# A two-layer diffusion trunk on one core: last squares summed by TensorE, two items tile by tile, low parts in halves, and a new order of the second attention

## The chip, the core and the metric

The kernel runs on one core of a Trainium2 chip. Its engines work side by side and wait for each other through semaphores: TensorE (PE in the profile: matrix products into eight PSUM banks), VectorE (DVE) and ScalarE (ACT) for elementwise work, GpSimd (POOL) likewise, and SyncE (SP), which issues most DMAs. Each engine takes its instructions strictly in the order in which they were written. The metric is the device time of one execution in microseconds, 2162.36 us (median of three runs, 2161.0 to 2166.12).

## The reference

256 latent tokens and 256 context tokens of width 1024 pass two layers in fp32. A layer is a half-step SwiGLU feed-forward (width 2816), then three mixers side by side (latent attention "MLA" with 8 heads, differential attention with 8 heads, pooling over windows 2 to 16) whose outputs are gated, summed and projected, then a second half-step feed-forward. Cut to what matters here:

```
def rmsnorm(x, g):
    y = x32 * rsqrt(mean(x32 * x32, axis=-1) + EPS);  return y * g
for l in range(2):
    x = x + 0.5*m[2] * swiglu(rmsnorm(x, g0)*(1+m[1]) + m[0], *ffa)      # h (context) alike
    sx = mixer_streams(rmsnorm(x, g1)*(1+m[4]) + m[3], ...)              # keys of h and x together
    x = x + m[5] * mixer_output(sx, keys_x, ...)                         # h only in layer 0
    x = x + 0.5*m[8] * swiglu(rmsnorm(x, g2)*(1+m[7]) + m[6], *ffb)      # h only in layer 0
return rmsnorm(x, final_g)
```

What follows turns on the line between two parts: every norm needs the sum of squares of all 1024 channels of a token, and the next products can start only when the normed values are there.

## The kernel before

Activations lie transposed: eight tiles `X[k]` of 128 channels x 512 tokens, columns 0 to 255 the latent stream (X), 256 to 511 the context stream (H). Every product is made of three passes in a reduced fp32 format (`mm3`, line 301): an operand is split into a high part and a low part (`hi`, `lo`; `uh`, `ul`), and high x high, high x low and low x high are summed in PSUM. One weight block of 128x128 with one stream of 256 columns is thus three matmuls.

Weights come as 406 chunks of 128x1024 (eight blocks each) in the order of use. For each chunk (`Weights.split`, from line 140) SP loads `w`, ACT writes `hi` (line 152), and GpSimd or VectorE (by the flag `on_pool`) subtracts to get `lo` (line 156). A ring of four chunks limits how far this runs ahead.

The parts of a layer meet in `boundary` (from line 466). Half of the last product is made for both streams; the last four output tiles are made first for H, then for X, from the same held weights. Every finished tile is added to `X[k]` on VectorE (line 619 or 1404), squared on ACT and accumulated into `acc` on GpSimd (`sqacc`, from line 357); only the last tile's square is added by VectorE. `stat` (line 381) sums `acc` over the partitions on TensorE into `pst`; a square root and a reciprocal follow, `bcast` (line 396) spreads the result by two transposes into the PSUM tile `rB`, and `modulate` (lines 409 to 419) makes `uh` and `ul` for each of the eight tiles (a DVE, an ACT and a DVE instruction). The statistics of H come early, while X is still being made. After the last X tile, the next part's first items (`head()`) run for H: `fg` and `fu` of two feed-forward slices, or `dk0`, `dq0` and the values `dv0` of the attention (tiles `it`, `it`, `vi`). Item 0 runs alone over its eight blocks, then comes the statistic of X, then item 1, with `bcast` of X in its middle; then the other H items, and at last all items for X.

There are four such boundaries: into the attention of layer 0, into its second feed-forward, into layer 1's first feed-forward, into the attention of layer 1. The next ones, into layer 1's last feed-forward and to the end, use other code.

The mixing part walks over twelve attention units in layer 1: eight differential ones (head pair j, query tile qt), then four of MLA. A unit's scores (`a1`, four PSUM banks `sc`) and softmax (`soft`: four maxima on DVE, four exponentials `pe` on ACT) are written at once; the rest of the queue of each engine is set by hand in `SCHEDULE` (from line 44), one string per layer, one field between bars behind each unit. In it `N` is a step of normalising, `T` the transposes of the oldest pending unit, `V` its product with the values, `P` and `D` send low parts to GpSimd or VectorE, and names are fillers: projections (`dk2`, `cq1`, `q5`, `kr`), gate products (`g41`: output tile 4, branch 1), statistics (`ls`, `sq`, `st`), norms (`nk0`, `dn3`), pooling (`p1`, `pp1`, `pj1`). The four score banks, `tr`, `po`, `it` and `gt` tiles all come from the same ring of eight banks.

Of the kernel before, what the change touches and what calls it, by code (L numbers as in the profile page):

```python
# [17 lines left out]
D = 1024  # L18
KD = 8
T = 512  # L20
# [5 lines left out]
X_, H_ = 0, 1  # L26
XC, HC = slice(0, 256), slice(256, 512)
# [28 lines left out]
)  # L56


# [26 lines left out]
class Weights:  # L85
# [54 lines left out]
    def split(self, n, parts, copy):  # L140
        k, nc = self.k, self.k.nc
        hi = k.wpool.tile([128, CW], F32R, tag="hi", name=f"hi{n}", bufs=RING)
        lo = k.wpool.tile([128, CW], F32R, tag="lo", name=f"lo{n}", bufs=RING)
        if n in self.early:
            d = self.early.pop(n)
            nc.sync.dma_start(hi.bitcast(F32), d[:, 0, :])
            nc.sync.dma_start(lo.bitcast(F32), d[:, 1, :])
            self.hi[n], self.lo[n] = hi, lo
            return
        raw = k.raw_tile(f"w{n}")  # L150
        nc.sync.dma_start(raw, self.stream[n])
        copy(hi, raw)  # L152
        eng = nc.gpsimd if k.pool_split(n) else nc.vector
        for p in range(parts):
            c = slice(p * CW // parts, (p + 1) * CW // parts)
            eng.tensor_tensor(out=lo[:, c], in0=raw[:, c], in1=hi[:, c].bitcast(F32), op=ALU.subtract)  # L156
        self.hi[n], self.lo[n] = hi, lo
# [2 lines left out]
        floor = self.c if self.floor is None else min(self.floor, self.c)  # L160
        self.prefetch(floor + self.look)

    def prefetch(self, n, parts=1, copy=None):
        while self.done < NSPLIT and self.done <= n:
            self.split(self.done, parts, copy or self.k.nc.scalar.copy)
            self.done += 1
# [24 lines left out]
class Kernel:  # L191
# [274 lines left out]
    def boundary(self, l, i, specs, xs, update, head, func):  # L466


        nc = self.nc
        self.norm_begin(l, i)  # L470
        ng = 4
        cols = ALLC
        for dm, p in self.gemms(specs, xs, cols, range(KD - ng)):
            update(dm, p, cols)
            self.sqacc(dm, cols)
        self.preload(AF.Sqrt)
        W = self.W
        was, self.on_pool = self.on_pool, True
        W.hold()
        g = range(KD - ng, KD)  # L480
        blks, banks = {}, {}
        for dm in g:
            banks[dm] = self.ps("dn")
            blks[dm] = self.gemm(banks[dm][:, HC], specs(dm), xs, HC)
            update(dm, banks[dm], HC)
            self.sqacc(dm, HC, nc.vector if dm == KD - 1 else None)
        mids = (None, lambda: (self.bcast(H_), self.mod_list(H_, (0, 1))),
                lambda: self.mod_list(H_, (4, 5)), lambda: self.mod_end())
        ends = ((), (2, 3), (6, 7), ())
        for n, dm in enumerate(g):  # L490
            self.gemm(banks[dm][:, XC], blks[dm], xs, XC, mids[n])
            update(dm, banks[dm], XC)
            self.sqacc(dm, XC, nc.vector if dm == KD - 1 else None)
            if n == 0:
                self.stat(H_)
            self.mod_list(H_, ends[n])
            W.release(blks[dm + 1][0] if dm + 1 < KD else None)
        W.hold()
        items = head()

        def xstat():
            self.stat(X_)
            self.preload(func)
        for n, it in enumerate(items):
            it.mm(H_, lambda: (self.bcast(X_), self.mod_list(X_, range(KD)), self.mod_end()) if n == 1 else None)
            if n == 0:
                xstat()
        two = [it for it in items if not isinstance(it, Kernel.VItem)][:2]
        rest = [it for it in items if it not in two]
        preps = [it.prep(X_) for it in two]  # L510
        blks = [[] for _ in two]
        for k in range(KD):
            for (out, specs, xs, cols), bs in zip(preps, blks):
                b = specs[k] if not isinstance(specs[k][0], str) else W.take(specs[k])
                bs.append(b)
                self.mm3(out, b[:2], tuple(x[:, cols] for x in xs[k]), k == 0, k == KD - 1)
        for n, it in enumerate([None] + rest):
            if it:
                it.mm(X_)
            W.release(rest[n].blks[0] if n < len(rest) else None)  # L520
            self.run_later()
            for x in (it,) if it else two:
                x.finish()
        self.on_pool = was
# [39 lines left out]
    class FFN:  # L564
# [7 lines left out]
        def head(self):  # L572
            return [Kernel.FItem(self, f, up) for f in range(2) for up in (False, True)]
# [36 lines left out]
        def specs(self, fs):  # L610
            return lambda dm: [(self.down, self.l, f * 128, ((dm * 128, 128),)) for f in fs]

        def update(self, dm, p, cols):
            K, nc = self.K, self.K.nc
            m = 3 * self.i + 2
            for s in (X_, H_):
                if SC[s].start >= cols.start and SC[s].stop <= cols.stop:
                    x = K.X[dm][:, SC[s]]
                    nc.vector.scalar_tensor_tensor(out=x, in0=p[:, SC[s]], scalar=K.mod(self.l, m, s, dm), in1=x,  # L619
                                                   op0=ALU.mult, op1=ALU.add)  # L620
# [1149 lines left out]
```

## Time and profile before

| | us |
|---|---|
| median of three runs | 2162.36 |
| the profiled execution | 2161.61 |
| its span in the trace | 2159.8 |
| busy in the span: PE, DVE, ACT, POOL | 2120.6, 1370.3, 899.7, 772.2 |

TensorE is busy for 98% of the span. What any change of order can give back is the rest, and the stretches in which its granted clock is at the lower of its two levels (the mean over the execution is 0.991 of full speed). The profile's table by stretches shows where both lie; the list of waits says what PE waited for; the chain of waits and the engines' timelines say why that came late.

### The profile page before, as it was taken

How to read it: one execution, taken by the hardware profiler on the slowest of the kernel's cores; microseconds unless marked ns; L12 is line 12 of the kernel's file. 1: busy time of each engine (PE TensorE's matmuls, PEld its weight loads, DVE VectorE, ACT ScalarE, POOL GpSimd, SP SyncE). 2: the span in 40 equal slices, each digit the busy share in tenths (PEclk: the TensorE clock that was granted, in tenths of full speed). 3: DMA queues.
4: the chain of work that ended last, by engine and by line, in shares of the span. 5: the costliest groups of instructions: out<-in, count | busy, mean ns of one | idle time of the engine just before them, and what ended most of it. 6: DMA issues, size and time to landing. Idle time of an engine off the chain costs nothing.

```text
span 2159.8 us, 31295 instructions
## 1 busy us (share of the span) xinstructions
PE 2120.6 (98%) x12032; PEld 1824.9 (84%) x12032; DVE 1370.3 (63%) x2016; ACT 899.7 (42%) x1529; POOL 772.2 (36%) x561
## 2 busy tenths in 40 slices
PE   9999999999999999999999999999999999999998
PEld 5888888977887788888888898888889888999998
DVE  6665655456656799468758745544534776667755
ACT  4433233345565533432212243332333557555544
POOL 0333324322475411555545544333343347301000
PEclk9999999999999999999999999999999999999999
DMA  7577767264322466245444515786664552455653
GB/s 265 184 292 278 256 265 273 86 217 142 113 93 80 150 234 234 88 145 181 172 166 166 175 69 209 294 299 237 264 246 147 205 185 79 166 200 191 229 183 115
DMA packets 119241, 408.91 MB, mean 189 GB/s; under 512 B 13234, under 2 KB 16946, under 8 KB 119092
## 3 DMA queue, kind: packets, MB, share of 16 engines
q1 hardware_dynamic: 103252, 354.48, 46.7%
q10 hardware_dynamic: 15840, 52.44, 6.2%
q8 instruction: 94, 1.54, 0.3%
q14 instruction: 55, 0.45, 0.1%
HBM read 348.67 MB, written 58.20 MB: 188 GB/s over the span
## 4 chain that ended last, share of the span: by engine, by line
PE 86%; DVE 6%; ACT 4%; issue 1%; DMA 1%; POOL 1%; ACTq 0%; DVEq 0%; SPq 0%; POOLq 0%
PE dn L301 22%; PE fu L301 19%; PE fg L301 19%; PE gt L301 8%; PE it L301 5%; PE br L301 5%; PE vi L301 2%; ACT pe L806 1%; DVE ul L419 1%; PE fg L1578 1%; PE fu L1578 1%; PE pa L1508 1%; PE tr L853 1%; PE sc L1118 1%; DMA X<-X 1%
## 5 line engine op out<-in xcount | busy, mean ns | idle before, releaser
L156 POOL TENSOR_TENSOR lo<-w,hi 128x1024 fp32r<-128x1024 f32 x204 | 530.4, 2603 | 701.3 <-ACT hi L152 652.9
L152 ACT CAST hi<-w 128x1024 fp32r<-128x1024 f32 x359 | 374.8, 1049 | 579.2 <-DMA w<-in_stream 237.6
L271 DVE CUSTOM_DVE_ANT_0 junk<-a,cvec 128x1024 bf16<-128x1024 f32 x224 | 400.5, 1788 | 3.7
L301 PE MATMUL dn<-hh,hi 128*128 128x512 f32 (+1 forms) x800 | 272.7, 341 | 0.0
L301 PE MATMUL dn<-hl,hi 128*128 128x512 f32 (+1 forms) x800 | 272.2, 340 | 0.0
L301 PE MATMUL dn<-hh,lo 128*128 128x512 f32 (+1 forms) x800 | 272.2, 340 | 0.0
L156 DVE TENSOR_TENSOR lo<-w,hi 128x1024 fp32r<-128x1024 f32 x155 | 190.5, 1235 | 127.9 <-ACT hi L152 125.5
L301 PE MATMUL fg<-ul,hi 128*128 128x512 f32 (+2 forms) x712 | 252.4, 354 | 1.6 <-DVE ul L419 1.6
L301 PE MATMUL fu<-uh,hi 128*128 128x512 f32 (+2 forms) x712 | 253.8, 357 | 0.0
L301 PE MATMUL fu<-ul,hi 128*128 128x512 f32 (+2 forms) x712 | 253.2, 356 | 0.0
L301 PE MATMUL fu<-uh,lo 128*128 128x512 f32 (+2 forms) x712 | 253.1, 355 | 0.0
L301 PE MATMUL fg<-uh,hi 128*128 128x512 f32 (+2 forms) x712 | 251.7, 354 | 0.0
L301 PE MATMUL fg<-uh,lo 128*128 128x512 f32 (+2 forms) x712 | 251.5, 353 | 0.0
L301 PEld LDWEIGHTS dn<-hh,hi 128*128 128x128 f32 x800 | 151.7, 190 | 17.0
L301 PEld LDWEIGHTS dn<-hl,hi 128*128 128x128 f32 x800 | 151.7, 190 | 16.8
L301 PEld LDWEIGHTS dn<-hh,lo 128*128 128x128 f32 x800 | 151.7, 190 | 16.9
L619 DVE SCALAR_TENSOR_TENSOR X<-dn,md,X 128x256 f32<-128x256 f32 x112 | 50.2, 479 | 170.6 <-PE dn L301 170.5
L301 PEld LDWEIGHTS fg<-ul,hi 128*128 128x128 f32 x712 | 134.4, 189 | 21.1 <-DVE ul L419 2.8
L301 PEld LDWEIGHTS fu<-uh,hi 128*128 128x128 f32 x712 | 136.4, 192 | 18.5
L301 PEld LDWEIGHTS fu<-ul,hi 128*128 128x128 f32 x712 | 136.4, 192 | 18.4
L301 PEld LDWEIGHTS fu<-uh,lo 128*128 128x128 f32 x712 | 136.2, 191 | 18.3
L301 PEld LDWEIGHTS fg<-uh,lo 128*128 128x128 f32 x712 | 134.5, 189 | 18.5
(321 smaller groups left out, 4303.2 us busy)
## 6 DMA issues: line engine op xcount, KB each, us to landing
w<-in_stream SPq DMA_DIRECT2D x359, 512.0 KB, 4.2
a<-in_ada SPq DMA_DIRECT2D x136, 512.0 KB, 4.4
el<-in_stream SPq DMA_DIRECT2D x47, 512.0 KB, 3.7
early<-eh ACTq DMA_DIRECT2D x47, 512.0 KB, 2.7
early<-el ACTq DMA_DIRECT2D x47, 512.0 KB, 3.7
hi<-early SPq DMA_DIRECT2D x47, 512.0 KB, 4.4
lo<-early SPq DMA_DIRECT2D x47, 512.0 KB, 5.8
a<-in_stream SPq DMA_DIRECT2D x8, 512.0 KB, 6.6
```

Source lines behind the costliest of these rows:

```text
L152: copy(hi, raw)
L156: eng.tensor_tensor(out=lo[:, c], in0=raw[:, c], in1=hi[:, c].bitcast(F32), op=ALU.subtract)
L271: nc.vector.tensor_tensor_reduce(out=self.junk, in0=raw, in1=self.cvec[:, s, :], scale=1.0, scalar=0.0, op0=ALU.mult, op1=ALU.add, accum_o ...
L301: nc.tensor.matmul(out, a, b, start=first and n == 0, stop=last and n == 2)
L419: self.nc.vector.scalar_tensor_tensor(out=lo, in0=t, scalar=sh, in1=hi.bitcast(F32), op0=ALU.add, op1=ALU.subtract)
L619: nc.vector.scalar_tensor_tensor(out=x, in0=p[:, SC[s]], scalar=K.mod(self.l, m, s, dm), in1=x, op0=ALU.mult, op1=ALU.add)
L806: nc.scalar.activation(e[:, c], banks[i][:, c], AF.Exp, bias=nm[:, o:o + 1], scale=1.0, accum_out=ls[:, o:o + 1])
L853: nc.tensor.transpose(t[:, i * 128:i * 128 + 128], P[:, i * 128:i * 128 + 128], self.ident)
L1118: nc.tensor.matmul(out[qt], a[0:96, q0:q0 + 128], b[0:96, kc], start=n == 0, stop=n == 2)
L1508: nc.tensor.matmul(pa[0:2, c], ccol[:, 2 * i:2 * i + 2], ada[k, m][:, i * 128:i * 128 + 128], start=i == 0, stop=i == KD - 1)
L1578: nc.tensor.matmul(b, w[n // 2], x, start=k == n == 0, stop=k == KD - 1 and n == 2)
```

## The change

Four edits:

- In `boundary` the square of the last tile isn't added to `acc` any more. `stat` sums two tiles instead of one: `acc` (seven squares) and the last square, each with its own matmuls.
- The first two items of the next part, where both have an H half and neither makes values, run block by block in turn for H. The statistic of X stands after the sixth block pair, the spreading of X after the eighth, and then come the other H items. The boundary into the attention of layer 1 keeps the old order: its items are `dk0`, `dv0`, `dq0`, and `dq0` there has no H half.
- A low part made on GpSimd is written as two instructions of 512 columns (VectorE's stay whole).
- The string of layer 1 in `SCHEDULE` is another permutation of fillers; `g32` and `g22` are no longer pulled forward, `g10`, `g20` and `g50` are.

```diff
@@ SCHEDULE, layer 1 (the first of its lines)
-    "N dk1 dq1 | N P kv0 cq0 | N | N N N N N T kv1 N N N V D dk2 N N N dq2 N T N N N | N N cq1 | N cq2 dk3 N N P "
+    "dk1 dq2 N | N P N N N dq1 cq0 kv0 | P N T kv1 N | N N | dk2 N N N N D N N dk3 N N T N N dq3 cq1 N N N V N "
...
@@ Weights.split
         eng = nc.gpsimd if k.pool_split(n) else nc.vector
+        if eng is nc.vector:
+            parts = 1
...
-    def prefetch(self, n, parts=1, copy=None):
+    def prefetch(self, n, parts=2, copy=None):
...
@@ boundary (for H and for X alike)
-            self.sqacc(dm, HC, nc.vector if dm == KD - 1 else None)
+            self.sqacc(dm, HC, False if dm == KD - 1 else None)
...
-        for n, it in enumerate(items):
-            it.mm(H_, lambda: (self.bcast(X_), self.mod_list(X_, range(KD)), self.mod_end()) if n == 1 else None)
-            if n == 0:
-                xstat()
+        def xmods():
+            self.bcast(X_)
+            self.mod_list(X_, range(KD))
+            self.mod_end()
+        pair = [it for it in items if not isinstance(it, Kernel.VItem) and H_ in getattr(it, "streams", (H_,))][:2]
+        if len(pair) == 2:
+            preps = [it.prep(H_) for it in pair]
...
+            for k in range(KD):
+                for (out, sp, ys, cols), it in zip(preps, pair):
+                    it.blks.append(W.take(sp[k]))
+                    self.mm3(out, it.blks[k][:2], tuple(x[:, cols] for x in ys[k]), k == 0, k == KD - 1)
+                if k == 5:
+                    xstat()
+                elif k == 7:
+                    xmods()
+            for it in items:
+                if it not in pair:
+                    it.mm(H_)
+        else:
+            for n, it in enumerate(items):
+                it.mm(H_, xmods if n == 1 else None)
+                if n == 0:
+                    xstat()
```

TensorE's queue at the boundary into the second feed-forward of layer 0, before: the last block of `fg` (weights `hi`, `lo`; streamed halves `uh`, `ul`), the statistic of X, the first block of `fu`.

```order
L301 MATMUL fg<-uh_8078,hi_8043 128x256
L301 MATMUL fg<-ul_8079,hi_8043 128x256
L301 MATMUL fg<-uh_8078,lo_8044 128x256
L381 MATMUL pst<-pick,acc 128x2 x2
L301 MATMUL fu<-uh_8064,hi_8111 128x256
L301 MATMUL fu<-ul_8065,hi_8111 128x256
L301 MATMUL fu<-uh_8064,lo_8112 128x256
```

The same place in the changed kernel, around the sixth block pair:

```order
L303 MATMUL fu<-uh_8147,hi_8184 128x256
L303 MATMUL fu<-ul_8148,hi_8184 128x256
L303 MATMUL fu<-uh_8147,lo_8185 128x256
L383 MATMUL pst<-pick,acc 128x2 x2
L383 MATMUL pst<-pick,sq 128x2 x2
L303 MATMUL fg<-uh_8149,hi_8184 128x256
L303 MATMUL fg<-ul_8150,hi_8184 128x256
L303 MATMUL fg<-uh_8149,lo_8185 128x256
```

The statistic stands behind twelve blocks instead of eight, and has twice the matmuls.

ScalarE's queue in layer 1's attention around the squares of the differential heads (`sq<-od`), before: they follow the exponentials of the eleventh unit, and the square root of the statistic (`r`) that needs them comes right after.

```order
L1140 ACTIVATE pe,ls<-sc,nm 128x512 x4
L884 COPY pv<-po 64x512
L340 CAST pth<-tr 128x4x128 x4
L152 CAST hi_15700<-w_15702 128x1024
L993 COPY pp<-it 128x256
L1140 ACTIVATE pe,ls<-sc,nm 128x512 x4
L952 ACTIVATE sq<-od_14127 128x256
L952 ACTIVATE sq<-od_14128 128x256
L952 ACTIVATE sq<-od_14129 128x256
L952 ACTIVATE sq<-od_14130 128x256
L349 ACT_TABLE_LOAD
```

Now:

```order
L1163 ACTIVATE pe,ls<-sc,nm 128x512 x4
L907 COPY pv<-po 64x512
L975 ACTIVATE sq<-od_14325 128x256
L975 ACTIVATE sq<-od_14326 128x256
L975 ACTIVATE sq<-od_14327 128x256
L975 ACTIVATE sq<-od_14328 128x256
L342 CAST pth<-tr 128x4x128 x4
L152 CAST hi_15943<-w_15945 128x1024
L1016 COPY pp<-it 128x256
L1163 ACTIVATE pe,ls<-sc,nm 128x512 x4
L152 CAST hi_16021<-w_16023 128x1024
L1296 COPY sg<-gt 128x256
```

The squares stand before the transposes' casts and the exponentials, and the gate product `g50` now stands before the statistic on TensorE.

TensorE at the end of that attention, before: the last block of the pooling branch (`br` with `oph`, `opl`), the spreading for the norm of head pair 2 (`rb`), and at once the differential branch (`odh`, `odl`).

```order
L301 MATMUL br<-opl_16362,hi_16329 128x256
L301 MATMUL br<-oph_16361,lo_16330 128x256
L975 MATMUL rb_16536<-r_15790,cst 128x256
L301 MATMUL br<-odh_16487,hi_16329 128x256
L301 MATMUL br<-odl_16488,hi_16329 128x256
```

Now:

```order
L303 MATMUL br<-opl_16646,hi_16516 128x256
L303 MATMUL br<-oph_16645,lo_16517 128x256
L998 MATMUL rb_16751<-r_16062,cst 128x256
L303 MATMUL gt<-uh_13910,hi_16516 128x256
L303 MATMUL gt<-ul_13911,hi_16516 128x256
```

The 24 matmuls of the gate `g01` moved from before the pooling projection `pj0` to between that norm and the branch that needs it.

## Rows read from the trace of the kernel before

**Rows 1.** Table by stretches: start:end, length, then busy us, PEclk, DMA share, GB/s.
```profile
393.00:436.00 43.00, 41.16 (x316) 38.65 (x316) 24.31 (x63) 16.80 (x36) 10.04 (x9) 1.00 0.41 143
...
888.00:929.00 41.00, 37.46 (x282) 36.67 (x282) 23.43 (x41) 19.54 (x34) 16.99 (x10) 0.92 0.19 65
...
1258.00:1298.00 40.00, 36.47 (x282) 35.67 (x281) 22.82 (x41) 19.61 (x34) 16.39 (x9) 0.91 0.20 75
...
1628.00:1662.00 34.00, 32.16 (x260) 31.27 (x259) 21.01 (x47) 14.47 (x30) 10.05 (x9) 1.00 0.34 114
1662.00:1936.00 274.00, 261.92 (x1922) 237.95 (x1921) 186.63 (x306) 152.51 (x317) 106.58 (x126) 0.98 0.50 175
```

**Rows 2.** Waits of PE, 888 to 930 us: us in total, times, longest.
```profile
PE pst L381 <- DVE acc L371: 2.7, 1, 2.7
PE fg L301 <- DVE ul L419: 0.8, 2, 0.6
```

**Rows 3.** Chain of waits, 888 to 930 us: start, us, what.
```profile
888.60 0.34 PE pst L381 x4
...
893.82 0.39 DVE ut L409
894.21 0.40 DVE ul L419
...
896.93 2.32 DVE ul L419
...
902.37 0.43 ACT sq L367
...
902.89 2.12 DVE acc L371
...
905.15 0.99 PE pst L381 x4
906.14 2.77 PE fu L301 x12
...
909.33 2.41 PE fu L301 x12
```

**Rows 4.** Chain of waits, 393 to 440 us.
```profile
410.41 1.45 PE it L301 x12
```

**Rows 5.** Timeline of PE, 888 to 933 us: start, us, instruction.
```profile
897.73 0.28 PE L301 MATMUL fg<-uh,hi 128*128 128x256 f32 x1
```

**Rows 6.** Timeline of POOL, 890 to 914 us: start, us, instruction, idle before.
```profile
896.56 2.41 POOL L156 TENSOR_TENSOR lo<-w,hi 128x1024 fp32r<-128x1024 f32 x1 [1.36 <-ACT hi L152]
...
902.38 4.84 POOL L156 TENSOR_TENSOR lo<-w,hi 128x1024 fp32r<-128x1024 f32 x2 [1.35 <-ACT hi L152]
```

**Rows 7.** Groups by line and form: POOL's 512-column sum.
```profile
L371 POOL TENSOR_TENSOR acc<-acc,sq 128x512 f32<-128x512 f32 x12 | 15.5, 1294 | 17.7 <-ACT sq L367 17.6
```

**Rows 8.** Waits of PE, 1655 to 1940 us.
```profile
PE sc L1118 <- ACT qh L343: 3.6, 1, 3.6
PE st L961 <- ACT sq L952: 2.1, 1, 2.1
PE tr L853 <- ACT pe L806: 1.6, 1, 1.6
PE rb L938 <- DVE r L915: 1.2, 1, 1.2
PE br L301 <- DVE odl L341: 1.1, 1, 1.1
PE it L301 <- DVE pdl L341: 1.1, 1, 1.1
PE gt L301 <- ACT pe L806: 0.7, 1, 0.7
```

**Rows 9.** Timeline of DVE, 1824 to 1862 us.
```profile
1847.11 1.45 DVE L341 TENSOR_TENSOR pdl<-po,pdh 128x256 fp32r<-128x256 f32 x1
```

**Rows 10.** Timeline of POOL, 1824 to 1862 us.
```profile
1845.89 4.89 POOL L156 TENSOR_TENSOR lo<-w,hi 128x1024 fp32r<-128x1024 f32 x2 [1.37 <-ACT hi L152]
```

More of the change, by code (lines that the diff above doesn't have):

```diff
@@ L492, in boundary @@
             update(dm, banks[dm], XC)
-            self.sqacc(dm, XC, nc.vector if dm == KD - 1 else None)
+            self.sqacc(dm, XC, False if dm == KD - 1 else None)
             if n == 0:
@@ L503, in xstat @@
             self.preload(func)
-        for n, it in enumerate(items):
-            it.mm(H_, lambda: (self.bcast(X_), self.mod_list(X_, range(KD)), self.mod_end()) if n == 1 else None)
-            if n == 0:
-                xstat()
+        def xmods():
[5 more added lines that the diff above has]
+            preps = [it.prep(H_) for it in pair]
+            for it in pair:
+                it.blks = []
+            for k in range(KD):
[14 more added lines that the diff above has]
+                    xstat()
         two = [it for it in items if not isinstance(it, Kernel.VItem)][:2]
```

8 rows, old and new, of the table SCHEDULE are left out of this document.

## The prediction

> **What bounds the kernel now.** I read the profile in this order. First its engine shares: PE is busy for 98% of the span, so nothing that shortens VectorE, ScalarE or GpSimd counts unless PE waits for it. Second, the table by stretches [rows 1], which is to show where PE's idle time lies. The feed-forward stretches have none. The four boundaries that the change touches have 1.84 (43.00 - 41.16), 3.54, 3.53 and 1.84 us. The attention of layer 1 has 12.08 (274.00 - 261.92). The granted clock is full (1.00) in the first and fourth boundary and 0.92 and 0.91 in the two before a feed-forward; it is 0.98 over layer 1's attention. Third, PE's waits and the chain at a boundary [rows 2, 3]. At 888 to 930 us PE waits 0.8 us in two pieces for the last low parts `ul`, and then 2.7 us for the sum of squares: the last square is ready on ScalarE at 902.80 (902.37 + 0.43), but VectorE's adding it takes 2.12 us. While PE waits, the clock falls: the four matmuls of the statistic take 0.99 us where the same four took 0.34 a moment before, and twelve matmuls take 2.77 and, part of them at the old clock again, 2.41 us. Where the clock stays up, twelve take 1.45 [rows 4], which is 0.12 us for one. These are the two levels, 1.2 and 2.4 GHz. Fourth, the waits of layer 1's attention [rows 8].
>
> **The change part by part: the boundaries.** The sum VectorE did (2.12 us here) leaves the path between the last square and the statistic. In its place `stat` gets four more matmuls, 0.34 us by the row of the same four at full clock [rows 3]; two statistics in each of four boundaries make 8 x 0.34 = 2.7 us, all on PE, since PE is what ends there.
>
> Taking two items together changes the pace at which PE eats `uh` and `ul`. One block used to be three matmuls (0.36 us); now six (0.72 us). The rows of `ul` waits [rows 2] say that at 0.36 us PE ran into VectorE, which here makes a pair of `ut` and `ul` in 0.79 us (0.39 + 0.40 [rows 3]). At 0.72 us, starting at 897.73 (the first `fg` matmul of before [rows 5]; the end of the X tiles doesn't move), the sixth pair ends at 897.73 + 6 x 0.72 = 902.05. By then the wait for `ul` should be gone. The statistic needs the square by 902.0 and it comes at 902.80, if nothing on VectorE or ScalarE gets earlier: 0.8 us of waiting are left of 3.5.
>
> The halves on GpSimd bear on this. A low part takes GpSimd 2.41 us [rows 6], and a VectorE instruction that reads two SBUF tiles and starts inside it is stretched to its end: `ul` from 896.93 takes 2.32 us and ends at 899.25, the low part at 898.97 [rows 3, 6]. Where two low parts stand back to back [rows 10], VectorE's `pdl`, begun at 1847.11, ends at 1848.56, just behind the first of them (half of 4.89 us, so 1848.34), while the second runs on [rows 9]. So VectorE gets in where one GpSimd instruction ends, and with halves it finds such a place after 1.29 us at most (the 512-column sum on GpSimd [rows 7]) instead of 2.41. There are two such stretches between the statistics of H and the last X tile of this boundary, so up to 2 x 1.1 us are saved; I expect about one, which would close the 0.8 us. The Trainium skill says of this pair of ports (SBUF — State Buffer, "Who interferes with whom") that whichever instruction comes first holds them whole and the other one blocks. That agrees with the stretched `ul`; but it also speaks against the halves: between two of them a VectorE instruction can take the ports and GpSimd then waits. By that, a low part would get later by one VectorE instruction, and the weights of the boundary with it; taken alone this would leave the 0.8 us in place in both feed-forward boundaries, and the gain summed below would be 0.8 us smaller.
>
> Cost of the halves themselves: 2 x 1.29 against 2.41 to 2.45 us, so 0.13 to 0.17 us more GpSimd time for each low part. It is hidden wherever GpSimd is idle, as in the feed-forwards, where PE has no idle time at all. If it wasn't, it would have to come out in the attentions. Do the weights of the third item come in time, when PE reaches them 7 us earlier than before? The chain needs them at 902.0 + 0.7 (statistic) + 1.4 (two pairs) = 904.2; the two low parts that begin at 902.38 [rows 6] give the first half of the third item's chunk at about 903.7 and its second half at 905.0, used only from 905.6. It fits by half a microsecond.
>
> After the statistic stand 12 matmuls (1.45 us) before the spreading, as before; at 393 us, at full clock, PE had no wait there. Behind the spreading stand two full H items (5.8 us) instead of two and a half. The first X `ul` comes within 2 us of the spreading (0.39 + 0.40 and ScalarE's part between them), the eighth 7 x 0.79 = 5.5 later; PE wants the first after 5.8 us and the eighth 5.0 after that. No wait.
>
> So, by boundary: the second loses 3.54 of idle time and the clock's price, (0.99 - 0.34) + (2.77 - 1.45) + (2.41 - 1.45) = 2.93, and pays 0.68: -5.8. The third, where the clock comes back earlier, loses 3.53 and the first two of these terms, 1.97, less 0.68: -4.8. The first and fourth -1.84 + 0.68 = -1.2 each; the fourth keeps its item order, and gets this from the missing sum and the earlier `ul` alone. Together -12.9. For what is left of the wait at the statistic I add 0.4 us in each of two: **-12.1 us**. Bounds: -12.9, and -2.7 if half of the 10.75 us of idle time stays, the clock falls as before and the 2.7 us of added matmuls are paid.
>
> **The attention of layer 1.** Of the waits [rows 8], I go through the new order. (a) 2.1 us, statistic for the squares: the squares now stand a unit earlier on ScalarE and `g50` (24 matmuls, 2.9 us) before the statistic; gone. (b) 1.1 us, differential branch for `odl`: `g01` moves there with 2.9 us; gone. (c) 0.7 us, gate for a score bank: more work lies before the same bank of the ring; gone. (d) 3.6 us, scores of the second MLA unit for `qh`: the field before it (`mb q3 T q5 k2`) has the same fillers, since the dropped `V` was one that does nothing; stays. (e) 1.6 us, transposes for a score bank: two units stood close behind one another; now it is the third and fourth, and `dk2` takes the wait; stays. (f) 1.2 us, `nk0` for the reciprocal: a product of 16 matmuls (1.9 us) goes from the cover, but the softmax in front of it on VectorE starts some 2 us earlier, as no projections stand between the fifth and sixth unit; stays, between 0 and 3.1. (g) 1.1 us, `pj0` for `pdl`: one gate before it instead of two (-2.9 us of cover), but less in VectorE's queue; stays, between 0 and 4. Gone are 3.9 us. A new order also makes waits that I don't see; I put 1.0 for them. The mean clock of 0.98 means that 0.02 x 274 = 5.5 us are lost to the low level in this stretch [rows 1]; I leave that as it is. **-2.9 us**, bounds -14 (waits and clock both mended but for (d)) and +8.
>
> The attention of layer 0 keeps its order; the rest of the span, it included, has 39.2 - 22.8 = 16.4 us of PE idle time (2159.8 - 2120.6 less the five stretches). I put 0 for what the halves do there, between -2 and +2.
>
> **Sum.** 2161.6 - 12.1 - 2.9 = 2146.6 on the profiled execution (span 2159.8 and 1.8 around it). It lies 0.75 us under the median of three, so on that scale it is 2147.4. I forecast **2147**.
>
> **The rivals.**
> 1. The boundaries mend, but the new order of the attention costs: (f) and (g) grow by 1.9 and 2.9 us, and each is followed by a low clock as the boundary's was (about 2 us): 8.8 - 3.9 = +4.9 instead of -2.9. 2162.4 - 12.1 + 4.9 = 2155. For it: the cover is shorter in both places; against: VectorE's queues are shorter too.
> 2. The wait only moves: the statistic waits for the square behind ScalarE's cast of weights, PE pauses and the clock falls all the same; half of the boundaries' gain: 2162.4 - 6.0 - 2.9 = 2153.5. For it: the 0.8 us left by the times of before; against: a wait of that size kept the clock up at 393 us.
> 3. Order and halves better than I see: the attention gets -10 to -14, 2137 to 2140. For it: three of its waits go for certain, and with them perhaps low-clock stretches; against: (d) and (e).
> 4. Slower. The mechanism is the ring of eight banks: each differential unit takes four, and they come free only as the exponentials do. If in the new order five more places wait as (e) did, 1.6 us, with 2 us of low clock, that is 18 us against 15 won: 2162.4 - 12.1 - 2.9 + 18 = 2165. It decides from four such places on. Against: one field of nearly nothing stands in both orders, and the new one has more work than before between most other units.
>
> **How the numbers follow.** The forecast with its small changes (2143 to 2151) has 0.50, the first rival 0.17, the second 0.10, the third 0.16, the fourth 0.07. The range is 2138 to 2157. Faster by over 0.3% (below 2155.9; about what a measurement of this kernel can tell from no change) comes from the forecast and the third rival whole, two thirds of the first and second: 0.84. Within 0.3%: 0.11. Slower: 0.05.
>
> **What would show it.** In the changed kernel's table, the two feed-forward boundaries should have under 1 us of PE idle and a clock of 1.00, and the eight matmuls of each statistic 0.7 us. The chain there should go from X tile to square to statistic without `acc`. VectorE's `ul` should no longer take 2.3 us, but at most 1.8. In layer 1's attention the waits for `sq` and the `odl` of the branch should be missing, the wait for `qh` still there with 3 to 4 us. I'd be wrong if the clock fell at the boundaries after shorter waits, if PE waited for `lo` of the third item, or if a new wait of over 3 us stood in that attention.

## The result, and the profile after

The changed kernel takes 2141.92 us (median of four runs, 2138.65 to 2143.52) against 2162.24 us (median of four, 2161.0 to 2166.12): a ratio of 0.9901, 95% interval 0.9884 to 0.9918. The forecast was 2147 us; the range held the time, but the gain is 20.3 us where 15.0 were summed up. The profiled execution took 2142.41 us (span 2140.6).

The table by stretches of the kernel after, at the places of [rows 1] (start:end, length, busy us of PE, PEld, DVE, ACT and POOL with the instructions in brackets, then PEclk, DMA share, GB/s):

```profile
393.00:436.00 43.00, 43.00 (x335) 40.98 (x334) 22.61 (x62) 16.68 (x36) 10.58 (x11) 1.00 0.49 166
884.00:926.00 42.00, 42.00 (x323) 40.62 (x322) 24.03 (x46) 22.84 (x38) 25.80 (x20) 1.00 0.26 90
1248.00:1288.00 40.00, 40.00 (x313) 38.92 (x313) 20.67 (x42) 21.89 (x37) 22.95 (x19) 1.00 0.34 119
1612.00:1645.00 33.00, 32.89 (x266) 32.14 (x266) 19.81 (x47) 14.88 (x32) 10.58 (x11) 1.00 0.38 125
1645.00:1916.00 271.00, 259.75 (x1919) 236.35 (x1918) 175.30 (x304) 152.30 (x316) 108.71 (x142) 0.98 0.51 176
```

In three boundaries length and PE's busy time are equal: the idle 1.84, 3.54 and 3.53 us are gone, and the fourth keeps 0.11 of 1.84. The clock is 1.00 in all of them, where it was 0.92 and 0.91 in the second and third. POOL has 25.80 busy us in the second boundary where [rows 1] has 16.99, and the chain below waits for none of it. Only the last row, layer 1's attention, still idles (11.25 us) and runs below full clock.

The chain of waits at the second boundary, which answers to [rows 3] (start, us, what):

```profile
884.26 0.79 PE pst L383 x8
885.05 1.53 PE dn L303 x12
...
886.80 7.21 PE dn L303 x60
894.01 0.36 PE fg L303 x3
894.37 0.36 PE fu L303 x3
...
897.97 0.36 PE fu L303 x3
898.33 0.79 PE pst L383 x8
899.12 0.46 PE fg L303 x3
...
900.87 2.88 PE fg L303 x24
```

Before, the chain ran here over VectorE (`ut`, `ul`), the square and VectorE's adding. Now every piece is PE's own: no engine is waited for from the last `dn` products into the feed-forward. Each statistic is eight matmuls in 0.79 us where four took 0.34 [rows 3].

PE's waits from 1640 to 1935 us, which answer to [rows 8] (total us, times, longest):

```profile
PE sc L1141 <- ACT qh L345: 3.8, 1, 3.8
PE it L303 <- ACT pdh L342: 2.1, 1, 2.1
PE rb L961 <- DVE r L938: 1.4, 1, 1.4
PE tr L876 <- DVE kl L343: 0.9, 1, 0.9
PE it L303 <- ACT pe L829: 0.9, 1, 0.9
PE it L303 <- ACT pe L1163: 0.7, 1, 0.7
PE tr L876 <- DVE mv L343: 0.7, 1, 0.7
```

The waits for `sq` and for the `odl` of the branch are gone, `qh` stands, and the pooling projection's wait for `pdl` (1.1) has become one of 2.1 for `pdh`.

To compare kernels I cut each trace at fixed points of the program: the first of the `dn` products ahead of a boundary, and the first scores of layer 1's attention. Every time below is the difference of two such start times, so a boundary's row holds the feed-forward behind it too. "Entry and attention 0" is the first boundary with layer 0's attention. The short names are those of the experiments below.

| us | before | after | halves off (e1) | only halves (e2) | only pair (e4) | only unadded (e5) | pair + unadded (e8) | only order (e11) |
|---|---|---|---|---|---|---|---|---|
| entry and attention 0 | 495.37 | 490.73 | 490.84 | 493.16 | 491.15 | 494.39 | 490.60 | 494.37 |
| second boundary | 207.17 | 200.65 | 200.70 | 203.08 | 204.38 | 202.23 | 200.69 | 207.06 |
| third boundary | 206.40 | 200.63 | 200.68 | 201.57 | 204.33 | 202.11 | 200.70 | 206.36 |
| fourth boundary | 77.49 | 76.23 | 76.89 | 75.78 | 78.97 | 76.96 | 76.95 | 77.48 |
| attention 1 | 266.64 | 264.45 | 264.85 | 268.78 | 271.59 | 270.48 | 267.07 | 261.22 |
| PE idle, second boundary | 3.54 | 0 | 0 | 1.60 | 2.85 | 0.55 | 0 | 3.53 |

After less before, the rows give -4.64, -6.52, -5.77, -1.26 and -2.19. The stage behind the last attention is 1.03 us longer, all the rest 0.16: together -19.2, the difference of the spans (2159.8 - 2140.6). The noise of such a row can be seen in e11, whose program up to the row of attention 1 is that of before: 0.1 at the middle boundaries, 1.0 in the first row (1.5 longer up to the first scores, with 1.7 us lost to the clock there, and 2.5 shorter behind them). The stretch ahead of the first boundary isn't in the table. PE's first feed-forward product starts at 23.9 to 24.3 us in six of the thirteen profiles and at 25.8 in seven, for the changed kernel itself at 24.2 here and at 25.8 in its second profile (e9): totals of single executions that differ by 1.6 us say nothing of an edit.

### The profile page after: what moved, and what is told of

It is laid out like the page before. It is cut to its first block, busy times and chain, and to the rows that moved or that the text cites. A ratio compares the mean times of both kernels' runs of the same rounds, so it can differ in the third digit from the quotient of the medians.

```text
span 2140.6 us, 31721 instructions
## 1 busy us (share of the span) xinstructions
PE 2114.6 (99%) x12064; PEld 1822.2 (85%) x12064; DVE 1294.6 (60%) x2007; ACT 900.4 (42%) x1530; POOL 879.9 (41%) x767
## 4 chain that ended last, share of the span: by engine, by line
PE 89%; ACT 4%; DVE 4%; issue 1%; DMA 1%; POOL 1%; ACTq 0%; DVEq 0%; SPq 0%; POOLq 0%
PE dn L303 23%; PE fu L303 18%; PE fg L303 18%; PE gt L303 9%; PE it L303 7%; PE br L303 5%; PE vi L303 2%; ACT pe L829 1%; PE tr L876 1%; PE sc L1141 1%; PE fg L1601 1%; PE fu L1601 1%; PE pa L1531 1%; DVE lo L158 1%; PE po L900 1%
## 5 line engine op out<-in xcount | busy, mean ns | idle before, releaser
L158 POOL TENSOR_TENSOR lo<-w,hi 128x512 fp32r<-128x512 f32 x410 | 641.8, 1590 | 587.1 <-ACT hi L152 582.8
L273 DVE CUSTOM_DVE_ANT_0 junk<-a,cvec 128x1024 bf16<-128x1024 f32 x224 | 352.8, 1575 | 3.7
L603 DVE TENSOR_TENSOR h<-sg,fu 128x512 f32<-128x512 f32 x66 | 45.2, 686 | 190.6 <-PE fu L303 158.7
L303 PEld LDWEIGHTS fg<-uh,hi 128*128 128x128 f32 x712 | 134.4, 189 | 18.4
```

The source lines that it names most:

```text
L273: nc.vector.tensor_tensor_reduce(out=self.junk, in0=raw, in1=self.cvec[:, s, :], scale=1.0, scalar=0.0, op0=ALU.mult, op1=ALU.add, accum_o ...
L303: nc.tensor.matmul(out, a, b, start=first and n == 0, stop=last and n == 2)
L603: nc.vector.tensor_tensor(out=h[:, c], in0=sg[:, c], in1=pu[:, c], op=ALU.mult)
```

## The experiments

Theory A, with which I began: the halves let VectorE in earlier, and the boundaries need that. Rival B: the unadded squares and the pair suffice, and the halves do nothing on PE's path. For layer 1's attention the question was whether the new order or the clock moved it.

**e1: the change without the halves.**

```diff
-    def prefetch(self, n, parts=2, copy=None):
+    def prefetch(self, n, parts=1, copy=None):
```

> The changed kernel with whole low parts on GpSimd; everything else as changed (2141.9 us). Theory A: the halves give VectorE twice as many places to get in. Then without them the attention of layer 0 goes from 415.3 us (first scores to the next part's last product) back to some 417.9, and at the two feed-forward boundaries the statistic waits 0.5 to 0.9 us for the last square: 2145 to 2148 us in all. Theory B: the halves do nothing on PE's path, and layer 0's attention gained because its start moved against the weights' stream: 415.3 stays, no wait at the boundaries, 2141 to 2143.

Measured: 2144.76 us (2144.07 to 2145.56), ratio 0.9908 (0.9893 to 0.9923). The time lies between the ranges of the two theories; the stages decide. Layer 0's attention stays short and no wait comes at the statistics, as B has it: second and third boundary are within 0.05 us of the full change, the fourth is 0.66 longer with 0.57 us of idle time. The rest of the 3.2 us between the two profiled spans is mainly 1.6 at the start, 0.4 in the attention of layer 1 and 0.4 behind it. The mechanism of the halves is there all the same: VectorE's `ul` of the second boundary, without halves and with them (timelines of DVE; start, us, instruction, idle before).

```profile
894.40 2.33 DVE L421 SCALAR_TENSOR_TENSOR ul<-ut,md,uh 128x256 fp32r<-128x256 f32 x1 [0.26 <-ACT uh L414]
```

```profile
892.72 1.20 DVE L421 SCALAR_TENSOR_TENSOR ul<-ut,md,uh 128x256 fp32r<-128x256 f32 x1 [0.25 <-ACT uh L414]
```

The low part on GpSimd beside it ends at 896.44 whole; the first of two halves ends after 1.3 us. But nobody waits for the 1.1 us. Theory A falls for the full change.

**e2: the kernel before with the halves alone.**

```diff
+        if eng is nc.vector:
+            parts = 1
...
-    def prefetch(self, n, parts=1, copy=None):
+    def prefetch(self, n, parts=2, copy=None):
```

> The kernel before (2162.2 us) with low parts on GpSimd in halves, and nothing else. Theory A: layer 0's attention falls from 417.9 to 415 to 416 us; at the feed-forward boundaries VectorE's ul take at most 1.5 instead of 2.3 us and the adding of the last square at most 1.5 instead of 2.1, so that PE's idle time there goes from 3.5 to 1.5 to 2.5 us; the clock may or may not fall. 2153 to 2158 in all. Theory B: 2161 to 2164, stages as before.

Measured: 2149.33 us (2144.37 to 2152.84), ratio 0.9927 (0.9910 to 0.9945). Of the parts tried alone this one saves most, more than theory A expected (2153 to 2158), though layer 0's attention didn't fall to 416 us: behind its first scores it takes 417.2, before 417.8. VectorE's adding of the last square, stretched as `ul` was, falls from 2.12 [rows 3] to 1.05 us, and the wait for it at the second boundary from 2.7 [rows 2] to this (waits of PE):

```profile
PE pst L383 <- DVE acc L373: 1.6, 1, 1.6
```

**e3: the change with the old order of layer 1's attention.**

```diff
-    "dk1 dq2 N | N P N N N dq1 cq0 kv0 | P N T kv1 N | N N | dk2 N N N N D N N dk3 N N T N N dq3 cq1 N N N V N "
+    "N dk1 dq1 | N P kv0 cq0 | N | N N N N N T kv1 N N N V D dk2 N N N dq2 N T N N N | N N cq1 | N cq2 dk3 N N P "
...
```

> The changed kernel with the old order of the second attention. My theory: the new order by itself gives 1 to 2 us of the 2.2 us that this stretch (first scores to the last projection) lost, so it goes from 264.4 to 265.5 to 266.6; 2143 to 2145 in all. Rival: the 2.2 us are the halves' work as in layer 0's attention and the new order gives nothing or costs: 262 to 264.5, 2139.5 to 2142.

Measured: 2143.53 us (2142.0 to 2146.82), ratio 0.9902 (0.9887 to 0.9916). Boundaries as in the full change, attention 264.36 us against 264.45. From this one pair of profiles I took the order to give nothing; e9 to e11 correct that.

**e4: the kernel before with the pair alone; e5: with the squares unadded alone.**

```diff
+        pair = [it for it in items if not isinstance(it, Kernel.VItem) and H_ in getattr(it, "streams", (H_,))][:2]
...                                                                  (e4, with the loop over the pair)
-            self.sqacc(dm, HC, nc.vector if dm == KD - 1 else None)
+            self.sqacc(dm, HC, False if dm == KD - 1 else None)     (e5, for X too)
```

> The kernel before with the first two items block by block in turn, the last square still added by VectorE, low parts whole, old order of the attention. My theory: the waits for ul (0.8 us) go, but the statistic still waits for VectorE's sum, which comes at about 905.0 while PE is there at 902.05: 2.5 to 3 us of idle time and a fallen clock at each feed-forward boundary stay; 2157 to 2161 in all. Rival: filling PE with twelve blocks keeps the clock up, and each of the two boundaries loses 4 us or more: 2150 to 2153.

> The kernel before with the last square given to TensorE unadded, items one after the other, low parts whole, old order of the attention. My theory: at the feed-forward boundaries the statistic waits 0.6 to 0.8 us for the square (902.95 against 902.3) beside 0.8 us for ul; the clock stays up there; less 0.7 us for the added matmuls each of the two loses 4 to 5 us: 2151 to 2154 in all. Rival: pauses of 1.5 us within 3 us let the clock fall all the same: each loses 1 to 2 us, 2157 to 2160.

Measured: e4 2160.54 us (2155.48 to 2164.02), ratio 0.9981 (0.9970 to 0.9992); e5 2154.52 (2153.48 to 2160.74), ratio 0.9961 (0.9947 to 0.9975). Each leaves another part of the same wait. PE's waits at the second boundary, first e4, then e5:

```profile
PE pst L381 <- DVE acc L371: 2.9, 1, 2.9
```

```profile
PE fg L301 <- DVE ul L419: 0.5, 2, 0.3
```

The pair removes the waits for `ul` and keeps that for the sum, and the clock still falls; the unadded square removes the sum, keeps the waits for `ul`, and the clock stays up. The wait of 0.6 to 0.8 us for the square that I expected in e5 didn't come. Of e5's 4.94 us at this boundary 2.99 are idle time; the rest is the clock, less the added matmuls. Alone the three edits save 4.09, 2.79 and 4.94 us here, 11.8 together; the full change saves 6.52. They are three cuts at one wait.

**e8: pair and unadded squares together, without halves and with the old order** (from the change, e1's and e3's edits in one).

> The changed kernel with the old order of the attention of layer 1 and with whole low parts: only the unadded squares and the pair are left of the change. Theory P, the pair and the unadded squares carry the whole gain: no idle time of TensorE at the first three boundaries, about 0.5 us at the fourth, clock 1.00 there, and a time of 2143 to 2147 us, within 2 us of the whole change. Theory Q, the halves or the new order are needed beside them, each hidden behind the other in the runs that took away only one: over 2148 us, with idle time back at a boundary or with over 15 us of idle time in the attention of layer 1.

Measured: 2145.20 us (2144.04 to 2151.73), ratio 0.9920 (0.9903 to 0.9936). Its table by stretches:

```profile
393.00:436.00 43.00, 43.00 (x333) 40.90 (x333) 23.35 (x62) 16.68 (x36) 10.03 (x9) 1.00 0.50 166
884.00:926.00 42.00, 42.00 (x319) 40.53 (x319) 25.84 (x46) 22.73 (x38) 24.06 (x12) 1.00 0.32 102
1248.00:1288.00 40.00, 40.00 (x309) 38.85 (x309) 21.28 (x42) 22.38 (x38) 21.48 (x11) 1.00 0.37 122
1612.00:1645.00 33.00, 32.44 (x260) 31.54 (x260) 20.10 (x47) 14.58 (x31) 10.02 (x9) 1.00 0.37 123
```

Three boundaries without idle time, 0.56 us in the fourth: rival B holds but for that one. The time is 2.5 us over that of the whole change on the same chip (e9), where at most 2 were expected. Against its twin with halves (e10: 2143.98) it is 1.2 us slower by the medians; the ranges overlap, and the traces put 0.7 us of that into the fourth boundary.

**e6, e7: the wait for `qh`.** My theory was that `q3` is projected too late for its unit. e6 moves it two fillers ahead, e7 in addition exchanges `p0` and `g12`.

```diff
-... V N k1 ma N | mb q3 T q5 k2 | ... pj1 p2 g12 | ... p0 g11
+... V N k1 ma q3 N | mb T q5 k2 | ... pj1 p2 g12 | ... p0 g11     (e6)
+... V N k1 ma q3 N | mb T q5 k2 | ... pj1 p2 p0 | ... g12 g11     (e7)
```

> The changed kernel with the projection q3 moved one unit earlier (from behind mb to behind ma), so that it stands before the scores of the first MLA unit. My theory: the wait of 3.8 us for qh before the second MLA unit is the wait for one late projection, queued behind the first unit's maxima and exponentials; with it made earlier the wait falls under 1 us, and some of the low clock behind it goes: 2136 to 2139.5 us in all, 260 to 262 in the second attention. Rival: the same unit's four score banks hold the ring, so a wait for the exponentials takes its place; less than 1.5 us is won: 2140.5 to 2142.

> As the last one, and the pooling projection p0 changes places with the gate g12, two units earlier. My theory: the wait of 2.1 us for pdh before pj0 is due to GpSimd's pooling of p0 and what VectorE and ScalarE have queued before it; two units earlier it is ready, and a further 1.5 to 2.5 us are won against q3 moved alone. Rival: p0's pooling on GpSimd now delays the scaling of the probabilities or the queries of the last unit, and nothing is won (within 0.7 us).

Measured: e6 2146.78 us (2146.02 to 2148.09), e7 2153.63 (2150.31 to 2154.3): slower than the change, both, where my theories had them faster by 2 to 8 us and the rivals about level. PE's longest wait in e6's attention:

```profile
PE it L303 <- ACT pe L1163: 4.7, 1, 4.7
```

The 3.8 us are gone and 4.7 us stand elsewhere. The chain of e6 says what was behind them:

```profile
1750.74 4.65 DMA w<-in_stream
...
1757.98 1.30 POOL lo L158
...
1759.44 0.65 POOL pw L1024
...
1764.59 0.72 POOL qf L1106
1765.33 0.42 ACT qh L345
```

`qh` needs GpSimd's `qf`, and that stands behind a low part whose weights land at 1755.4 and behind a pooling sum. The chain of the changed kernel itself shows the like ahead of its 3.8 us:

```profile
1765.58 1.06 ACT hi L152
...
1767.93 1.27 POOL lo L158
...
1769.27 0.72 POOL qf L1106
...
1770.02 0.42 ACT qh L345
```

The projection's place on PE is not what held `qh` up; the theory falls. Whether another order of GpSimd's queue mends it wasn't tried.

**e9, e10, e11: the order once more.** e9 is the changed kernel, e10 the same with the old order (e3's program), e11 the kernel before with the new order alone; all on one chip.

> The changed kernel itself once more, to see how far its attention of layer 1 differs between two profiled executions. Theory P, the low-clock stretches follow from the waits and so from the program: the stretches stand at the same places (near 1713 and 1768 us), the stage takes 264.5 us within 0.5. Theory R, they come and go from run to run: another number of them, and the stage moves by 1.7 us for each 3.4 us of low clock. The time is 2142 us within 1.5 by both.

> The changed kernel with the old order of the attention of layer 1, once more, beside the changed kernel on the same chip. By the prediction's term for the order it is 2.9 us slower than the changed kernel. By theory P, the order gives nothing, the two agree within 1 us. Its first profile had two low-clock stretches of about 3.4 us in that attention; theory R says that this number changes.

> The kernel before with the new order of the attention of layer 1 alone. By the prediction's term 2.9 us faster than the kernel before (about 2159 to 2161 us, ratio 0.9987). By theory P nothing: within 1 us of the kernel before, with the boundaries' idle time of 1.84, 3.54, 3.53 and 1.84 us unchanged, and the waits for the squares and for the low parts of the differential heads gone but their time back elsewhere in the same stage.

Measured: e9 2142.67 us (2140.62 to 2147.66), e10 2143.98 (2143.67 to 2146.11), e11 2159.54 (2153.07 to 2167.0) against 2165.24 of the kernel before (2158.55 to 2170.91), ratio 0.9975 (0.9962 to 0.9988). So on the kernel before the order is worth 5.4 us (2.6 to 8.2). The attention of layer 1 in e9, then in e10:

```profile
1646.50:1908.50 262.00, 252.31 (x1864) 229.98 (x1864) 171.29 (x297) 147.94 (x308) 107.80 (x141) 0.99 0.53 178
```

```profile
1645.00:1912.60 267.60, 255.74 (x1866) 231.85 (x1865) 179.95 (x297) 147.79 (x307) 108.46 (x139) 0.97 0.51 173
```

Over all profiles of the two orders, the old takes 264.4 to 271.6 us (seven profiles, mean 268.1), the new 261.2 to 264.9 (four, mean 263.1). But three of the seven, e2, e4 and e5 (268.8 to 271.6), have no partner with the new order, so these 5.0 us hold other edits too. The sets that differ in the order alone are before against e11, e3 and e10 against the change and e9, and e8 against e1; their means:

| layer 1's attention, us | old order (before, e3, e8, e10) | new order (e11, after, e9, e1) |
|---|---|---|
| length, mean and range | 266.4 (264.4 to 267.6) | 263.1 (261.2 to 264.9) |
| PE idle | 12.0 (11.6 to 12.6) | 9.4 (8.1 to 11.3) |
| PE busy at the lower clock | 9.9 (6.6 to 13.0) | 9.6 (6.8 to 16.7) |

The order gains 3.3 us: 2.6 of idle time, whose ranges don't overlap (those of the lengths do, by 0.5 us), and 0.15 of clock (half of 0.3 us less at half speed); 0.6 is left over. One profile each, as in e3, can't show it, since the clock moves by itself: theory R. The changed kernel twice, first the profile shown above, then e9, whose start lies 1.6 us later:

```profile
1710.00:1715.00 5.00, 3.57 (x18) 2.14 (x17) 4.56 (x5) 2.86 (x7) 0.00 (x0) 0.88 0.00 0
1715.00:1720.00 5.00, 5.00 (x19) 2.81 (x18) 3.14 (x5) 1.61 (x3) 0.00 (x0) 0.78 0.00 0
...
1828.00:1833.00 5.00, 2.80 (x17) 1.94 (x16) 3.41 (x8) 2.38 (x6) 2.99 (x4) 1.00 0.28 105
```

```profile
1710.00:1715.00 5.00, 3.57 (x29) 3.35 (x28) 4.95 (x4) 3.98 (x8) 0.00 (x0) 1.00 0.00 0
1715.00:1720.00 5.00, 5.00 (x21) 2.53 (x20) 3.64 (x7) 1.51 (x4) 0.00 (x0) 1.00 0.00 0
...
1828.00:1833.00 5.00, 4.25 (x21) 3.59 (x22) 3.14 (x6) 2.52 (x6) 2.71 (x2) 0.79 0.44 134
```

The same program, the same wait of 1.4 us (up to 1713.1 and up to 1714.7), and the clock falls behind it once and once not; near 1830, behind a wait of 2.1 us in both, it is the other way about.

Why e9 is ahead of e10 by only 1.3 us of median is settled in part: in e9's profile the stage behind that attention takes 105.49 us against 104.42, as it does in the change (105.44) and in e1 (105.83). In the change PE has 0.25 us of idle time there and its weights come at 250 GB/s where e10 has 270. e11 with the new order alone has 104.4, and so have e6 and e7, the changed kernel with a filler or two moved. PE's weight loads wait there for low parts that VectorE makes, in two places: 0.6 us together in the change, 0.7 in e9, 1.1 in e1, none in e10. Why those come late is open.

## Why the prediction was right, and where it was not

- **The sum leaves the path: right; the waits for `ul` mis-sized.** No `acc` stands in the chain, the clock stays at 1.00, `ul` takes 1.20 and not 2.3 us. Second and third boundary gain 6.5 and 5.8 us where 5.4 and 4.4 were expected with the residual wait, the fourth 1.26 for 1.2 (0.66 of it by the halves, by e1). That is more than even the bound without a residual wait, 5.8 and 4.8: the term for the waits for `ul` was too small. I took the 0.8 us of idle time [rows 2]. But the 24 `fg` matmuls of before, 0.12 us apart at full pace, start over 4.43 us, from 897.73 [rows 5] to the last one's 902.16, where 23 x 0.12 = 2.76 would do; so 1.67 us lay in them. A matmul is shown as 0.28 us long though the next one can start 0.12 after it, and a wait shows as idle time only beyond that end.

```profile
902.16 0.28 PE L301 MATMUL fg<-uh,lo 128*128 128x256 f32 x1
```

- **The added matmuls: mis-sized.** Eight cost 0.79 us where four cost 0.34, so 0.45 for each statistic and not 0.34; 3.6 us over eight statistics, not 2.7.
- **The 0.8 us left at the statistic: failed.** The step took the last square at its old time, 5.07 us behind the first `fg` (902.80 - 897.73). In e1, without halves, it comes 4.68 behind (900.35 - 895.67; the timelines of PE and ACT below), and the first four matmuls of the statistic take `acc`, so the square is needed some 0.4 us later than I counted. There PE loses 0.06 us (the statistic takes 0.85). The halves bring it to 3.96 behind (897.80 - 893.84), where it is no longer needed.

```profile
895.67 0.28 PE L303 MATMUL fg<-uh,hi 128*128 128x256 f32 x1
899.93 0.42 ACT L369 ACTIVATE sq<-X 128x256 f32<-128x256 f32 x1
```

- **The halves: a part was right, their place in the sum was not.** I gave them the closing of a wait that was closed without them. In the full change the boundaries show them worth 0.7 us, at the fourth, which keeps its item order. Alone (e2) they would have been worth 4.1 us at the second. Their price was mis-sized: I took 2 x 1.29 us for a low part, 0.13 to 0.17 more than whole. Over the kernel a half takes GpSimd 1.590 us (410 of them, 641.8 us busy), where a whole took 2.603 (204, 530.4 us): 0.58 more for each. The rule of the Trainium skill (SBUF — State Buffer, "Who interferes with whom"), that GpSimd in turn waits where VectorE holds the ports, agrees with that, though no run here shows how much of the 0.58 such waits make; the 0.8 us that it would have cost at the statistic were not lost, since the square came early enough without the halves.
- **The attention of layer 0: failed.** I put 0 with bounds of 2 for it and -1.2 for its entry; together they gained 4.64 us, 2.0 up to the first scores and 2.6 behind them. Idle time gives 3.6 of it (1.84 + 5.76 = 7.60 before, 4.01 after). The step that failed is to let the gain of an entry end at its border: behind it the later scores waited for the first unit's exponentials. By the chain of before, these stood behind the write of an `X` tile to memory, whose landing ScalarE's queue (`ACTq`) awaited before it issued the next:

```profile
433.85 8.28 DMA X<-X
...
442.15 0.33 ACTq L1027
...
447.02 1.46 ACT pe L806 x4
...
448.52 0.96 PE sc L790 x6
```

  This DMA stands in the chains of before and of e2, where the part behind the first scores takes 417.8 and 417.2 us, and in no other. The nine profiles with the pair take 414.9 to 415.3 there. The pair isn't the only way to that: e11 has none and takes 415.2, after an entry that lost 1.7 us to the clock, and e5 takes 417.3, of which 1.7 is clock. What sets that landing is open.
- **The order of layer 1's attention: the term holds, not each wait.** I wrote -2.9 with the clock left as it was; idle time fell by 2.6 and the stage by 3.3, by the means of the pairs above. Gone as foreseen are (a) and (b); (d) stayed at 3.8 and (f) at 1.4. (g) doubled, within its bounds. Not seen: (c), which I had as gone, and (e) gave way to four waits of 0.7 to 0.9 us, one at 1675 us and three between 1759 and 1763. To leave the clock out was right on the mean (0.15 us), not for one profile.
- **Against the 1.03 us** that came back behind that attention stood no term.

Of the rivals, the first (order costs), the second (wait only moves) and the fourth (slower) are refuted by the stages above. The result is 5 us under the forecast and lies between forecast and third rival, but not for the third's reason: the surplus came at the boundaries and in layer 0's attention, not in layer 1's.

## What to carry to other kernels

Where an engine of the critical chain waits once and the clock falls behind the wait, several edits can each remove a large part of it (2.8 to 4.9 of 6.5 us here); price them one by one on top of the others, not each against the kernel before. Before an edit is credited with a wait, ask which of its companions already removes it. A stage whose clock wanders by itself needs several profiles of each version: one profile each (e3 and the change) had this order at 0.1 us, four of each at 3.3. And only versions that differ in nothing else belong into such a mean: with three more it would have read 5.0.

## What the runs showed of the hardware

- The granted clock falls to the lower level behind some waits and not behind others of the same length in the same program, 1.4 us at 1711 being one; in layer 1's attention the busy time at the lower level ran from 6.6 to 19.9 us over the eleven profiles of the two orders, for the changed kernel itself 8.2 and 6.8.
- A VectorE instruction of 0.40 us beside a GpSimd low part took 2.33 us, with the low part halved 1.20 us: it ends about when the GpSimd instruction under which it began ends, and the next one doesn't hold it up.
- Halving the low parts moved time from VectorE to GpSimd: where only the halves differ, VectorE's busy time falls from 1351.2 (e1) to 1294.6 us (change) and from 1370.3 (before) to 1312.6 (e2), and GpSimd's rises from 772.7 to 879.9 and from 772.2 to 885.6. GpSimd, now busy for 41% of the span, had room for it, and no boundary got longer. Its low parts before (whole) and after (halves), by groups (total us, mean ns, idle before them):

```profile
L156 POOL TENSOR_TENSOR lo<-w,hi 128x1024 fp32r<-128x1024 f32 x204 | 530.4, 2603 | 701.3 <-ACT hi L152 652.9 <-PE fg L301 25.9 <-PE fu L301 9.6
```

```profile
L158 POOL TENSOR_TENSOR lo<-w,hi 128x512 fp32r<-128x512 f32 x410 | 641.8, 1590 | 587.1 <-ACT hi L152 582.8 <-PE fu L303 4.0
```
